# Differential heads on one Trainium2 core: all of TensorE's work in one written order

## The chip, the cores and the metric

The kernel runs on one core of one Trainium2 chip. The metric is device time in microseconds (us) of one execution. The kernel before takes 2374.95 us, the median of three runs (2369.23 to 2376.01).

The engines of the core are named as in the profile: PE is TensorE (matmuls; PEld is its weight load), DVE is VectorE, ACT is ScalarE, POOL is GpSimd, SP is SyncE, which issues the transfers. Each takes its own queue of instructions, and they wait for each other through semaphores.

## The reference

One inference step of a backbone with two layers, for 128 context tokens and 128 latent tokens, all in float32. The first layer mixes by latent and grouped-query attention, the second by differential attention; each is followed by a gated convolutional feed-forward. Every sub-layer is modulated by a shift, a scale and a gate, which are products of a condition vector with `w_ada`. The change is in the second layer's mixer (`d` is 128, 8 heads):

```python
def diff_attention(q, k, v, lam, scale):
    def block(qb):
        s = jnp.einsum("bqhjd,bkhjd->bhjqk", qb, k).astype(jnp.float32) * scale
        p = jax.nn.softmax(s, axis=-1)
        a = (p[:, :, 0] - lam * p[:, :, 1]).astype(v.dtype)
        return jnp.einsum("bhqk,bkhd->bqhd", a, v)
...
def mixer_c(h, rope, ctx, layer_idx, w_in, lq1, lk1, lq2, lk2, g_sub, w_out):
    proj = h @ w_in
    ...
    q, k = apply_rope(q, cos_h, sin_h), apply_rope(k, cos_h, sin_h)   # latent tokens only
    ...
    o = diff_attention(q, k_all, v_all, lam, HEAD_SCALE)
    o = rmsnorm(o, g_sub) * (1.0 - lambda_init)
    return o.reshape(b, t, -1) @ w_out, new_ctx
```

The context tokens attend to themselves, the latent tokens to 128 cached keys and to themselves.

## The kernel before

Both groups of tokens go through the products together, 256 columns wide (`NT`). Activations lie with features on partitions. A product is made with three matmuls for each 128x128 block of weights: the weight is split into a high part `wh` (ACT's cast, line 222) and a low part `wl` (DVE's subtraction, line 223), the activation likewise (`xh`, `xl`), and `gemm` (line 308) sums `wh*xh`, `wh*xl` (lines 317 and 318) and `wl*xh` (line 321) over 16 blocks into a PSUM bank `acc`. These 48 matmuls are a chunk. Weights arrive in 1 MB loads (`raw`, three buffers); `wh` and `wl` have four buffers of eight blocks, two chunks together, so that a cast can start when the PE has used the block that lay there two chunks earlier.

In the differential mixer (`mixer_c`, line 951) a head has six chunks: two for its queries (`dq`), two for its keys (`dk`), two for its values. The first three chunks of head 0 are made earlier by `first_three`, 45 remain. `project` (line 969) copies a chunk out of PSUM (`dev`), rotates queries and keys on DVE (`rope`, line 640), and after the values transposes them (line 993). `attend` (line 1000) is a generator, one `yield` after each part:

- scores of both halves (line 1007), the maximum `dmx` on DVE (lines 657, 658), `nmx` on POOL, the exponentials on ACT, then on DVE `drec`, `nl` and four steps on `p` (lines 1013 to 1021)
- transposes of `p` (line 672) and ACT's copy `pT`
- the product with the values, `o` (lines 1026 to 1028); its squares on ACT, three steps on POOL (`var`), the scaled `on` on DVE (line 1041)
- transposes of `on` (line 1048), and their split into `oall`

`start` runs a generator to its first `yield`, `step` takes all running ones a step further. `pump` (line 529) is called after each chunk: it calls `step`, and then, at a rate of its own, the next steps of the conditioning product (`row_step`, line 492). A unit of that product is 128x512 blocks of `w_ada`, 16 of them. Most units are made on PE (`sum_rows`, line 441). Those in `SUMMED` are summed on DVE into `aacc` (`sum_block`, lines 453 to 461, 32 steps, each kept behind the DVE instruction that was written just before it); their partitions are then summed on PE (`reduce`, line 379). Both kinds end with ACT's copy `am` (`copy`, line 386) and transposes on PE (`turn`, line 393), whose result DVE adds into `mod`; `later` holds these last steps, and each `row_step` takes one of them.

The order of an engine's queue is not the written one: a scheduler lists instructions by readiness in its own estimate and by priority. `tc.keep_in_program_order(i)` holds one instruction behind the one that was written before it on the same engine. In `gemm` before, that is done only for the chunks that are given something to do in the middle (`between`); of the mixer's chunks these are two (`todo`). All other work of PE is put where the scheduler places it, in pieces, within chunks or between them.

Of the kernel before, what the change touches and what calls it, by code (L numbers as in the profile page):

```python
# [17 lines left out]
P = 128  # L18
D = 2048
KD = D // P  # L20
T = 128
# [68 lines left out]
def step_kernel(ctx: ExitStack, tc: tile.TileContext, A: dict):  # L90
    nc = tc.nc
    pe, dve, act, pool, sp = nc.tensor, nc.vector, nc.scalar, nc.gpsimd, nc.sync
# [50 lines left out]
    def load_cw(l):  # L143
        ada["cw"] = T_(keep, [P, 4, 2 * NFF], "convw")
        tc.keep_in_program_order(sp.dma_start(out=ada["cw"], in_=A["wconv"][:, l]))
# [141 lines left out]
    def first_three(W, xh, xl, order, mid=None, fixed=False):  # L287


        pin = tc.keep_in_program_order if fixed else lambda i: i  # L290
        raws = [W.load() for _ in range(3)]
        ps = [T_(pacc, [P, 512], "acc") for _ in range(3)]
        blocks = {(c, h): W.halves(raws[c], 8 * h) for c, h in ((0, 0), (1, 0), (2, 0), (0, 1))}
        count = [0] * 3
        for n, (c, k) in enumerate(order):
            if mid and n == len(order) // 2:
                mid()
            if (c, k // 8) not in blocks:
                blocks[c, k // 8] = W.halves(raws[c], 8)
            wh, wl = blocks[c, k // 8][k % 8]  # L300
            a, b = count[c] == 0, count[c] == KD - 1
            count[c] += 1
            pin(pe.matmul(ps[c][:, :NT], wh, xh(k), start=a, stop=False))  # L303
            pin(pe.matmul(ps[c][:, :NT], wh, xl(k), start=False, stop=False))  # L304
            pin(pe.matmul(ps[c][:, :NT], wl, xh(k), start=False, stop=b))  # L305
        return [p[:, :NT] for p in ps]

    def gemm(blocks, xh, xl, n=NT, first=0, between=None):


        fixed = lambda i: tc.keep_in_program_order(i) if between else i
        ps = T_(pacc, [P, 512], "acc")
        last = len(blocks) - 1
        for i in range(last + 1):
            k = (i + first) % (last + 1)
            wh, wl = blocks[k]
            fixed(pe.matmul(ps[:, :n], wh, xh(k), start=(i == 0), stop=False))  # L317
            fixed(pe.matmul(ps[:, :n], wh, xl(k), start=False, stop=False))  # L318
# [97 lines left out]
    def load_row():  # L416
        feat["row"] = T_(feat["home"], [P, 2, D], "condb")
        sp.dma_start(out=feat["row"], in_=A["condb"])
        for r in range(2):
            tc.keep_in_program_order(act.activation(feat["row"][:, r], feat["row"][:, r], AF.Silu))  # L420

    def feature_step():
# [7 lines left out]
        tc.keep_in_program_order(dve.tensor_tensor_reduce(  # L430
# [10 lines left out]
    def sum_rows(t, raw, ps=None):  # L441
        if t == 0:
            ada["ps"] = ps or T_(ppool["ada"], [P, 512], "ada", bufs=1)
        for g in range(4):
            i = pe.matmul(ada["ps"][32 * g:32 * g + 32, :], condw[:, 4 * t + g, :], raw[:, g],  # L445
                          start=(t == 0), stop=(t == 3), skip_group_check=True)
            if pinned[0]:
                tc.keep_in_program_order(i)
# [4 lines left out]
    def sum_block(acc, block, k):  # L453
        for c in range(2):
# [6 lines left out]
            tc.keep_in_program_order(i)  # L461
# [98 lines left out]
    def modulate(hx, rb, l, which, chunks, fixed=False):  # L560


        pin = tc.keep_in_program_order if fixed else lambda i: i
# [26 lines left out]
    def modulated(st, l, which, W, fixed):  # L590
# [31 lines left out]
        def turn():  # L622
            rest[1](tc.keep_in_program_order)
# [79 lines left out]
    def mixer_ab(hx, rb0, st):  # L703
        l = 0
        with tc.tile_pool(name="ab", bufs=1) as ab:
            with tc.tile_pool(name="abp", bufs=1) as pj:
# [7 lines left out]
                def caches():  # L714
                    tc.keep_in_program_order(sp.dma_start(out=ckc, in_=A["cache_ckv"]))
                    split(kv_in[:, :, 0, T:2 * T], kv_in[:, :, 1, T:2 * T], ckc)
                    tc.keep_in_program_order(sp.dma_start(out=kr[:, T:2 * T], in_=A["cache_krope"]))
                    tc.keep_in_program_order(sp.dma_start(out=kg[:, :, T:2 * T], in_=A["cache_gqa_k"]))
                    tc.keep_in_program_order(sp.dma_start(out=vg[:, 1], in_=A["cache_gqa_v"]))
# [231 lines left out]
    def mixer_c(cp, hx, W, ready, todo, st):  # L951
# [5 lines left out]
        tc.keep_in_program_order(pe.matmul(ps[:, 0:2], ones, lm, start=True, stop=True))  # L957
# [7 lines left out]
        product = lambda: ready.pop(0) if ready else gemm(W.chunk(), xh, xl, between=todo.pop(0) if todo else None)  # L965
# [3 lines left out]
        def project(h):  # L969
# [9 lines left out]
            for dst, to in ((q, T), (k, 2 * T)):  # L979
                for i in range(2):  # L980
                    ev = T_(cp, [P, NT], "dev", bufs=2)
                    act.copy(ev, product())
                    act.copy(dst[:, i, 0:T], ev[:, 0:T])
                    rope(dst[:, i:i + 1, to:], ev[:, None, T:], 1, 64, "rch", "rsh")
                    pump(rate)
            sp.dma_start(out=A["o_diff_k"][:, 2 * h:2 * h + 2], in_=k[:, :, 0:T])
            pt = T_(ppool["att"], [P, 512], "att", bufs=3)
            for i in range(2):
                ev = T_(cp, [P, NT], "dev", bufs=2)
                act.copy(ev, product())  # L990
                pump(rate)
                for g in range(2):
                    pe.transpose(pt[:, g * NT + i * P:g * NT + (i + 1) * P],
                                 ev[:, g * T:(g + 1) * T], ident)
            act.copy(v[:, 0], pt[:, 0:NT])
            act.copy(v[:, 2], pt[:, NT:])
            sp.dma_start(out=A["o_diff_v"][:, h], in_=v[:, 0])
            return q, k, v

        def attend(h, q, k, v):  # L1000
# [15 lines left out]
            for g, ks in ((0, slice(0, T)), (1, slice(T, 3 * T))):  # L1016
# [4 lines left out]
                                         op0=ALU.mult, op1=ALU.add)  # L1021
            yield
# [21 lines left out]
            yield  # L1044
            pt = T_(ppool["att"], [P, 512], "att", bufs=3)
# [6 lines left out]

        for h in range(8):
            start(attend(h, *project(h)))
# [16 lines left out]
    def ffn(hx, W, ready, todo, l, st):  # L1071
# [4 lines left out]
        with tc.tile_pool(name=f"ffn{l}", bufs=1) as fp, banks(f"pffn{l}") as pf:  # L1076
# [4 lines left out]
            def conv(m):  # L1081
                early = bool(ready)
                pin = tc.keep_in_program_order if early else lambda i: i
# [52 lines left out]
    with banks("pab") as ppool["ada"]:  # L1136
# [4 lines left out]
        half_unit(1, 0, first[1], tc.keep_in_program_order)  # L1141
# [4 lines left out]
        half_unit(0, 0, first[0], tc.keep_in_program_order)  # L1146
# [167 lines left out]
```

## Time and profile before

| | |
|---|---|
| median of three runs | 2374.95 us |
| the profiled execution | 2372.41 us |
| its span, first to last instruction | 2370.6 us |
| its mean granted clock of TensorE | 0.993 |
| differential heads, without their first chunks and the output product | 1236 to 1545 us of the span |

The page of the profile gives busy times of whole engines, a chain of waits and groups of instructions by line; `out<-in` names the tiles that an instruction writes and reads. A view of stretches gives each engine's busy time between two times, with the number of its instructions in brackets, the granted clock (`PEclk`), the share of the DMA engines and the GB/s. A timeline gives start, duration, engine, line, operation and tiles; `x8` merges eight instructions of a line that follow each other, and square brackets show the idle time of the engine just before and what ended it. Matmuls are pipelined: the start of the next tells more than the duration. On DVE, too, the next instruction starts some 0.08 us before the profile ends the one before it.

### The profile page before, as it was taken

Reading aid. Unit: us, or ns where it says so; the run is one execution under the profiler, and the core shown is the slowest. Engines: PE = TensorE matmul, PEld = TensorE weight load, DVE = VectorE, ACT = ScalarE, POOL = GpSimd, SP = SyncE. Lnnn points to the kernel's source line nnn. Section 1 sums busy time; section 2 is a strip of 40 time slices with the busy share of each in tenths; the row PEclk is TensorE's granted clock in tenths of the full one; section 3 lists DMA queues with packets and bytes.
Section 4 is the critical chain, followed back from the end, with each engine's and each line's share of the span. In section 5 each row is a group of like instructions: output and inputs, shape, how many; then the busy total and the mean of one; then the engine's idle time right before and its main releaser. Section 6 shows DMA issues by size and latency. Waiting matters only on the chain. (4 is left out here: it accounts for less than half of the span.)

```text
span 2370.6 us, 47563 instructions
## 1 busy us (share of the span) xinstructions
PE 2312.9 (98%) x19624; PEld 2189.4 (92%) x19624; DVE 1857.6 (78%) x2886; ACT 1165.7 (49%) x1857; POOL 179.7 (8%) x210
## 2 busy tenths in 40 slices
PE   6999999999999999999999999999999999999997
PEld 4688878899999999999989999998999999999997
DVE  3569868879999999999879887888899755666654
ACT  4345544465554355554465444446555434555543
POOL 0002211200000000001220100112000000000011
PEclk9999999999999999999999999999999999999999
DMA  9988777867777877777766787777677555555553
GB/s 370 365 306 300 291 292 263 325 223 257 267 267 275 308 265 259 263 259 274 284 232 243 286 292 278 280 292 273 246 260 259 208 196 196 194 193 191 192 194 123
DMA packets 99608, 612.95 MB, mean 259 GB/s; under 512 B 10752, under 2 KB 18624, under 8 KB 29632
## 3 DMA queue, kind: packets, MB, share of 16 engines
q1 hardware_dynamic: 99392, 609.92, 70.4%
q8 instruction: 154, 2.52, 0.4%
q14 instruction: 62, 0.51, 0.1%
HBM read 605.12 MB, written 4.75 MB: 257 GB/s over the span
## 5 line engine op out<-in xcount | busy, mean ns | idle before, releaser
L222 ACT CAST wh<-raw 128x1024 fp32r<-128x1024 f32 (+1 forms) x822 | 795.6, 979 | 914.8 <-PE acc L318 745.1
L223 DVE TENSOR_TENSOR wl<-raw,wh 128x1024 fp32r<-128x1024 f32 (+1 forms) x822 | 922.0, 1138 | 312.8 <-ACT wh L222 305.9
L317 PE MATMUL acc<-hx,wh 128*128 128x256 f32 x4064 | 1131.6, 279 | 4.1 <-ACT hx L583 3.0
L321 PE MATMUL acc<-hx,wl 128*128 128x256 f32 x4064 | 1125.5, 278 | 2.5 <-DVE wl L223 2.2
L318 PE MATMUL acc<-hx,wh 128*128 128x256 f32 x4064 | 1127.0, 278 | 0.0
L317 PEld LDWEIGHTS acc<-hx,wh 128*128 128x128 f32 x4064 | 763.6, 188 | 29.8 <-issue 14.5
L321 PEld LDWEIGHTS acc<-hx,wl 128*128 128x128 f32 x4064 | 762.4, 188 | 10.9 <-issue 3.8
L318 PEld LDWEIGHTS acc<-hx,wh 128*128 128x128 f32 x4064 | 764.3, 188 | 6.7 <-issue 5.4
L318 PE MATMUL acc<-g,wh 128*128 128x256 f32 x1408 | 388.3, 276 | 0.0
L321 PE MATMUL acc<-g,wl 128*128 128x256 f32 x1408 | 388.0, 276 | 0.0
L317 PE MATMUL acc<-g,wh 128*128 128x256 f32 x1408 | 387.8, 276 | 0.0
L430 DVE CUSTOM_DVE_ANT_0 junk<-araw,condb 128x2048 f32<-128x2048 f32 x120 | 274.6, 2288 | 0.0
L318 PEld LDWEIGHTS acc<-g,wh 128*128 128x128 f32 x1408 | 264.3, 188 | 0.0
L321 PEld LDWEIGHTS acc<-g,wl 128*128 128x128 f32 x1408 | 264.2, 188 | 0.0
L317 PEld LDWEIGHTS acc<-g,wh 128*128 128x128 f32 x1408 | 264.1, 188 | 0.0
L178 POOL TENSOR_TENSOR sqacc<-sqacc,sq 128x256 f32<-128x256 f32 x62 | 82.8, 1335 | 1520.2 <-issue 1215.8
L459 DVE SCALAR_TENSOR_TENSOR aacc<-araw,condw,aacc 128x512 f32<-128x512 f32 x150 | 111.0, 765 | 0.2
L1086 ACT ACTIVATE cv<-acc,convw 128x256 f32<-128x256 f32 x176 | 98.2, 558 | 5.3 <-PE acc L305 5.3
L459 DVE SCALAR_TENSOR_TENSOR aacc<-block,condw,aacc 128x512 f32<-128x512 f32 x120 | 90.0, 780 | 6.1 <-DMA block<-w_ada 6.0
L633 DVE SCALAR_TENSOR_TENSOR x<-acc,mod,x 128x128 f32<-128x128 f32 x192 | 57.8, 342 | 39.7 <-PE acc L321 37.4
L1089 DVE SCALAR_TENSOR_TENSOR cv<-acc,convw,cv 128x254 f32<-128x254 f32 x176 | 83.4, 474 | 5.2 <-ACT cv L1086 5.1
L1092 DVE SCALAR_TENSOR_TENSOR cv<-acc,convw,cv 128x254 f32<-128x254 f32 x176 | 84.2, 479 | 3.6
(240 smaller groups left out, 1976.5 us busy)
## 6 DMA issues: line engine op xcount, KB each, us to landing
raw<-w_up SPq DMA_DIRECT2D x176, 1024.0 KB, 4.8
araw<-w_ada SPq DMA_DIRECT2D x162, 1024.0 KB, 6.2
raw<-w_down SPq DMA_DIRECT2D x88, 1024.0 KB, 4.8
raw<-w_in_c SPq DMA_DIRECT2D x48, 1024.0 KB, 5.4
raw<-w_in_ab SPq DMA_DIRECT2D x19, 1024.0 KB, 5.7
block<-w_ada SPq DMA_DIRECT2D x64, 256.0 KB, 6.1
raw<-w_out_ab SPq DMA_DIRECT2D x16, 1024.0 KB, 7.6
raw<-w_out_c SPq DMA_DIRECT2D x16, 1024.0 KB, 6.1
```

The costliest lines, as they stand in the source:

```text
L178: eng.tensor_tensor(out=st["acc"], in0=st["acc"], in1=sq, op=ALU.add)
L222: pin(act.copy(out_hi, src))
L223: pin(dve.tensor_tensor(out=out_lo, in0=src, in1=out_hi.bitcast(F32), op=ALU.subtract))
L317: fixed(pe.matmul(ps[:, :n], wh, xh(k), start=(i == 0), stop=False))
L318: fixed(pe.matmul(ps[:, :n], wh, xl(k), start=False, stop=False))
L321: fixed(pe.matmul(ps[:, :n], wl, xh(k), start=False, stop=(i == last)))
L430: tc.keep_in_program_order(dve.tensor_tensor_reduce(out=T_(feat["pool"], [P, D], "junk"), in1=feat["row"][:, c], in0=feat["raw"].rearrange ...
L459: i = dve.scalar_tensor_tensor(out=acc[c], in0=block, scalar=condw[:, k, c:c + 1], in1=acc[c], op0=ALU.mult, op1=ALU.add)
L633: dve.scalar_tensor_tensor(out=x[:, c, s], in0=ps[:, s], scalar=mod[:, l, 3 * which + 2, c, g:g + 1], in1=x[:, c, s], op0=ALU.mult, op1=AL ...
L1086: pin(act.activation(y, ps, AF.Identity, scale=cw[:, 1, m:m + 1], bias=cw[:, 3, m:m + 1]))
L1089: pin(dve.scalar_tensor_tensor(out=y3[:, :, 1:], in0=p3[:, :, :T - 1], scalar=cw[:, 0, m:m + 1], in1=y3[:, :, 1:], op0=ALU.mult, op1=ALU.add))
L1092: pin(dve.scalar_tensor_tensor(out=y3[:, :, :T - 1], in0=p3[:, :, 1:], scalar=cw[:, 2, m:m + 1], in1=y3[:, :, :T - 1], op0=ALU.mult, op1=A ...
```

## The change

All of PE's instructions go through a small class. While `in_turn` is set, over the eight heads, each is kept behind the one written before it. `keep_order` is the old call, made once for an instruction. Each chunk of the mixer now has a `between`: in its middle come, in this order, what `todo` holds, `pump`, and what `soon` holds (the start of a head's `attend`, in its last value chunk). `attend` gets the value transposes as a part of its own, and one more `yield` before the last part, so that a head's steps stand in the middles of six chunks: scores, value transposes, transposes of `p`, `o`, none, transposes of `on`. `dev` has five buffers instead of two, since the value copies live longer.

```diff
-    pe, dve, act, pool, sp = nc.tensor, nc.vector, nc.scalar, nc.gpsimd, nc.sync
+    dve, act, pool, sp = nc.vector, nc.scalar, nc.gpsimd, nc.sync
+    kept = []
+
+    def keep_order(i):
+        if not any(i is j for j in kept):
+            kept[:] = [i]
+            tc.keep_in_program_order(i)
+
+    class TensorE:
+        in_turn = False
+        def matmul(self, *a, **kw):
+            return self.placed(nc.tensor.matmul(*a, **kw))
+        def transpose(self, *a, **kw):
+            return self.placed(nc.tensor.transpose(*a, **kw))
+        def placed(self, i):
+            if self.in_turn:
+                keep_order(i)
+            return i
+
+    pe = TensorE()
...
-        product = lambda: ready.pop(0) if ready else gemm(W.chunk(), xh, xl, between=todo.pop(0) if todo else None)
+        soon = []
+
+        def product(rate):
+            def middle():
+                if todo:
+                    todo.pop(0)()
+                pump(rate)
+                while soon:
+                    soon.pop(0)()
+            return ready.pop(0) if ready else gemm(W.chunk(), xh, xl, between=middle)
...
             for dst, to in ((q, T), (k, 2 * T)):
                 for i in range(2):
-                    ev = T_(cp, [P, NT], "dev", bufs=2)
-                    act.copy(ev, product())
+                    ps = product(rate)
+                    ev = T_(cp, [P, NT], "dev", bufs=5)
+                    act.copy(ev, ps)
                     act.copy(dst[:, i, 0:T], ev[:, 0:T])
                     rope(dst[:, i:i + 1, to:], ev[:, None, T:], 1, 64, "rch", "rsh")
-                    pump(rate)
             sp.dma_start(out=A["o_diff_k"][:, 2 * h:2 * h + 2], in_=k[:, :, 0:T])
-            pt = T_(ppool["att"], [P, 512], "att", bufs=3)
+            evs = []
             for i in range(2):
-                ev = T_(cp, [P, NT], "dev", bufs=2)
-                act.copy(ev, product())
-                pump(rate)
-                for g in range(2):
-                    pe.transpose(pt[:, g * NT + i * P:g * NT + (i + 1) * P],
-                                 ev[:, g * T:(g + 1) * T], ident)
-            act.copy(v[:, 0], pt[:, 0:NT])
-            act.copy(v[:, 2], pt[:, NT:])
-            sp.dma_start(out=A["o_diff_v"][:, h], in_=v[:, 0])
-            return q, k, v
+                if i:
+                    soon.append(lambda: start(attend(h, q, k, v, evs)))
+                ps = product(rate)
+                ev = T_(cp, [P, NT], "dev", bufs=5)
+                act.copy(ev, ps)
+                evs.append(ev)
 
-        def attend(h, q, k, v):
+        def attend(h, q, k, v, evs):
...
             yield
+            pt = T_(ppool["att"], [P, 512], "att", bufs=3)
+            for i, ev in enumerate(evs):
+                for g in range(2):
+                    pe.transpose(pt[:, g * NT + i * P:g * NT + (i + 1) * P],
+                                 ev[:, g * T:(g + 1) * T], ident)
+            act.copy(v[:, 0], pt[:, 0:NT])
+            act.copy(v[:, 2], pt[:, NT:])
+            sp.dma_start(out=A["o_diff_v"][:, h], in_=v[:, 0])
+            yield
             pT = transposed(cp, pj[0])
...
             yield
+            yield
             pt = T_(ppool["att"], [P, 512], "att", bufs=3)
...
+        pe.in_turn = True
         for h in range(8):
-            start(attend(h, *project(h)))
+            project(h)
+        pe.in_turn = False
         flush()
```

Elsewhere `tc.keep_in_program_order` becomes `keep_order`, with the same effect.

More of the change, by code (lines that the diff above doesn't have):

```diff
@@ L956, in mixer_c @@
         ps = att_bank()
-        tc.keep_in_program_order(pe.matmul(ps[:, 0:2], ones, lm, start=True, stop=True))
+        keep_order(pe.matmul(ps[:, 0:2], ones, lm, start=True, stop=True))
         ex = T_(cp, [P, 2], "ex")
@@ L1082, in conv @@
                 early = bool(ready)
-                pin = tc.keep_in_program_order if early else lambda i: i
+                pin = keep_order if early else lambda i: i
                 ps = product()
```

30 lines of the change are left out of this document (15 added, 15 removed).

## The prediction

> **What bounds the kernel now.** I read the page first.
>
> ```profile
> span 2370.6 us, 47563 instructions
> PE 2312.9 (98%) x19624; PEld 2189.4 (92%) x19624; DVE 1857.6 (78%) x2886; ACT 1165.7 (49%) x1857; POOL 179.7 (8%) x210
> PE 30%; issue 0%; DVE 0%; POOL 0%; ACT 0%; DVEq 0%; POOLq 0%; ACTq 0%
> ```
>
> TensorE (PE) is never out of work: busy 98%, and the only engine of weight on the chain that ended last. The change touches the differential heads, so the second view is the busy time by stretches: the whole stage, then the four stretches in which VectorE (DVE) sums a conditioning unit (`aacc`, lines 456 and 459), and one stretch between two of them.
>
> ```profile
> core 0: us, PE busy (x) PEld busy (x) DVE busy (x) ACT busy (x) POOL busy (x), PEclk, DMA share, GB/s
> 1236.00:1545.00 309.00, 309.00 (x2573) 287.94 (x2575) 252.27 (x456) 148.21 (x303) 26.56 (x40) 1.00 0.76 274
> 1251.32:1299.23 47.91, 47.91 (x415) 47.65 (x414) 47.22 (x82) 24.59 (x46) 2.93 (x5) 1.00 0.70 252
> 1299.23:1325.35 26.12, 26.12 (x206) 20.79 (x206) 14.20 (x27) 11.43 (x28) 2.55 (x5) 1.00 0.87 309
> 1325.35:1371.00 45.65, 45.65 (x391) 45.39 (x389) 45.34 (x80) 22.61 (x44) 4.77 (x5) 1.00 0.74 268
> 1398.70:1444.50 45.80, 45.80 (x386) 45.44 (x385) 45.48 (x80) 23.69 (x47) 5.43 (x6) 1.00 0.70 253
> 1472.10:1518.00 45.90, 45.90 (x391) 45.64 (x390) 45.49 (x82) 21.53 (x43) 4.05 (x5) 1.00 0.76 270
> ```
>
> PE is busy in every microsecond, so it waits for nothing here. But in the four summing stretches DVE is as full as PE: a unit takes DVE 46 to 48 us, whatever PE does. Between them DVE is half idle (14.20 of 26.12). PE does not wait only because what it needs from DVE stands late enough in its queue. The third view, DVE's timeline for one head inside such a stretch, shows how late, and gives the prices.
>
> ```profile
> 1277.34 1.47 PE L1007 MATMUL att<-dk,dq 128*128 128x128 f32 x8
> 1278.76 0.28 PE L318 MATMUL acc<-hx,wh 128*128 128x256 f32 x1
> ...
> 1279.65 0.28 DVE L657 TENSOR_REDUCE dmx<-att 128x1 f32<-128x128 f32 x1
> 1279.85 0.41 DVE L658 TENSOR_REDUCE dmx<-att 128x1 f32<-128x256 f32 x1
> 1280.18 1.21 DVE L223 TENSOR_TENSOR wl<-raw,wh 128x1024 fp32r<-128x1024 f32 x1
> ...
> 1285.75 0.17 DVE L1013 RECIPROCAL drec<-dsums 128x4 f32<-128x4 f32 x1
> ...
> 1287.72 0.59 DVE L648 TENSOR_TENSOR rope<-dev,cst 64x128 f32<-64x128 f32 x2
> 1288.32 0.29 DVE L650 TENSOR_TENSOR dq<-dev,cst 128x128 f32<-128x128 f32 x1
> 1288.53 0.74 DVE L459 SCALAR_TENSOR_TENSOR aacc<-araw,condw,aacc 128x512 f32<-128x512 f32 x1
> 1289.19 0.22 DVE L1015 TENSOR_SCALAR nl<-drec,nlam 128x2 f32<-128x2 f32 x1
> ...
> 1289.98 1.22 DVE L223 TENSOR_TENSOR wl<-raw,wh 128x1024 fp32r<-128x1024 f32 x1
> 1291.12 0.28 DVE L651 TENSOR_TENSOR dq<-dq,rope 128x128 f32<-128x128 f32 x1
> ...
> 1291.99 0.54 DVE L1017 TENSOR_SCALAR p<-p,nl 128x128 f32<-128x128 f32 x2
> ...
> 1295.83 0.74 DVE L1019 SCALAR_TENSOR_TENSOR p<-p,drec,p 128x128 f32<-128x128 f32 x2
> 1296.48 0.75 DVE L459 SCALAR_TENSOR_TENSOR aacc<-araw,condw,aacc 128x512 f32<-128x512 f32 x1
> ...
> 1299.60 0.41 PE L379 MATMUL ada<-aacc,cst 128*32 128x256 f32 x2
> ```
>
> Scores at 1277.34, the finished weights `p` at 1296.48: 19 us, over three chunks, since DVE takes its queue in turn. The sum of the unit is read by PE (line 379) at 1299.60, just as DVE ends it. From start to start the prices on DVE are: `aacc` step 0.66 (1288.53 to 1289.19), `wl` 1.14, a `dmx` pair 0.53, a `rope` pair 0.60, one `dq` or `dk` 0.21, the four `p` steps 1.11 (0.65 and 0.54 less the 0.08 by which neighbours overlap), `drec` and `nl` 0.22. As a test, the built order has 4 `dmx`, 5 `wl`, 10 `aacc`, 2 `rope` pairs, 3 `dq`, `drec`, `nl` and 4 `p` in this chain: 1.06 + 5.70 + 6.60 + 1.20 + 0.63 + 0.22 + 1.11 = 16.5 us, against 16.8 in the rows (1279.65 to 1296.48).
>
> **The change, part by part.** The written order is now PE's order. In the built program a chunk is 26 matmuls, one interruption, 22 matmuls; 76 interruptions over the stage become 42. Work is neither added nor removed: 2160 chunk matmuls in both. PE's prices:
>
> ```profile
> 1267.90 0.28 PE L317 MATMUL acc<-hx,wh 128*128 128x256 f32 x1
> ...
> 1272.66 0.28 PE L317 MATMUL acc<-hx,wh 128*128 128x256 f32 x1
> ```
> ```profile
> 1253.55 0.59 PE L1026 MATMUL att<-dv,pT 128*128 128x256 f32 x2
> ...
> 1254.96 0.28 PE L318 MATMUL acc<-hx,wh 128*128 128x256 f32 x1
> ```
> ```profile
> 1257.46 0.88 DVE L1041 SCALAR_TENSOR_TENSOR on<-att,var,cst 128x256 f32<-128x256 f32 x2 [0.28 <-POOL var L1038]
> ```
> ```profile
> 1260.30 0.60 PE L1048 MATMUL att<-cst,on 128*128 128x128 f32 x4
> 1260.66 0.37 PE L317 MATMUL acc<-hx,wh 128*128 128x256 f32 x1
> 1260.87 0.28 PE L318 MATMUL acc<-hx,wh 128*128 128x256 f32 x1
> ```
>
> 42 matmuls from 1267.90 to 1272.66 give 0.113 us each: 5.44 a chunk, 2.95 to its interruption, 2.49 after it. Scores cost 1.30 (1277.34 to 1278.76 less one matmul), `o` 1.30, four transposes 0.46. From the start of `o` to `on` on DVE it is 3.9 us (1253.55 to 1257.46, through ScalarE and three POOL steps); the `on` pair holds DVE 0.80.
>
> **Fewer interruptions.** A return to the chunk costs a matmul about 0.21 instead of 0.11 (1260.66 to 1260.87). If all 34 that go cost that, 3.4 us are saved; if the work merely moves, 0. I take 2.
>
> **Steps in turn on PE: the waits.** Anything that PE reaches before its operand is ready now holds back every matmul behind it. I set DVE's built order against PE's from a point where DVE must wait for PE (`dmx` after the first half of the scores, 0.65; `on` after `o`) to the point where PE needs DVE. `oall` (128x512) is taken as half a `wl`, 0.60.
>
> - Unit 1, its sum read in the first chunk of head 2. DVE from `on`: 0.80, 22 `aacc` 14.5, 8 `wl` 9.1, 2 `rope` pairs 1.2, 4 `dk` 0.8, `oall` 0.6, 4 `dmx` 1.06, `drec` and `nl` 0.22, 2 `p` 0.5: 28.8. PE from `o`: 1.30 + 2.49, 5.44, 5.44 + 0.46, 2.95 + 1.30 + 2.49, 2.95 + 0.46 = 25.3, less the 3.9 before `on`: 21.4. Wait 7.4.
> - Unit 3, the same places with 24 `aacc` and 4 `p`: 30.8 against 21.4. Wait 9.4.
> - Unit 2, first at `p` (second chunk of head 3): DVE 1.06, 5 `wl` 5.7, 10 `aacc` 6.6, 0.22, 0.6, 0.2, 1.11 = 15.5; PE 0.65 + 2.49 + 5.44 + 0.46 + 2.95 = 12.0. Wait 3.5. Then at the sum, from `p`: `o` after 0.35 + 2.49 + 2.95 = 5.8, `on` 3.9 later at 9.7, then 0.8, 8 `aacc` 5.3, 2 `wl` 2.3, 0.6, 0.4: 19.1; PE is there at 5.8 + 1.30 + 2.49 + 2.95 = 12.5. Wait 6.6.
> - Unit 4, first at `p`, 4 `wl` instead of 5: 14.4 against 12.0. Wait 2.4. Then at the sum: 9.7 + 0.8, 8 `aacc` 5.3, 4 `wl` 4.6, 1.2, 0.6, then `oall`, `dk` and 2 `aacc` 2.1: 24.3; PE 12.5 + 2.49 + 2.95 + 0.46 = 18.4 (one chunk later, behind the transposes of `on`). Wait 5.9.
>
> Together 35.2 us. What stands behind each wait is the chunk itself and, through the weight buffers that it frees, ScalarE's casts and SyncE's loads, so nothing else fills the time. In the old order PE's queue had the first unit's sum three chunks later, at the end of head 2's keys.
>
> **Copy and turn in one interruption.** In four interruptions the sum, ScalarE's copy of it (`am`) and the transposes of the copy now follow each other. The nearest row is the same sequence early in the program:
>
> ```profile
> 98.87 0.66 PE L393 MATMUL ada<-cst,am 128*128 128x128 f32 x4 [0.71 <-ACT am L386]
> ```
>
> ```profile
> 1287.22 1.06 ACT L222 CAST wh<-raw 128x1024 fp32r<-128x1024 f32 x1 [0.96 <-PE acc L318]
> ```
>
> 4 x 0.71 = 2.8, which I take, as ScalarE is half idle in this stage; if each copy first waits for a cast, 4 x 1.77 = 7. Below 0 it cannot come, since the transposes need the copy.
>
> **The clock after a wait.** PE's granted clock falls after an idle stretch:
>
> ```profile
> 1192.36:1195.78 3.42, 2.05 (x22) 1.95 (x24) 2.17 (x6) 1.46 (x3) 0.00 (x0) 1.00 0.30 71
> 1195.78:1199.19 3.41, 3.41 (x14) 0.80 (x18) 1.03 (x4) 0.00 (x0) 0.70 (x1) 0.50 0.87 198
> ```
>
> A window with 1.37 us idle was followed by 3.41 us at half clock, in which 1.7 us of progress are lost if PE has work. After the first waits of units 2 and 4 DVE uses that time and the second wait shrinks; four ends are left: 0 to 6.8, and 4 taken, as part of a half-clock window falls inside the wait. The Trainium skill (TensorE: Matmul & The Clock Gate, Part 1) says that the clock halves after at least one idle window of about 3.4 us. By that page the 2.4 us wait would cost no clock; the trace is stricter, since a window that was 60% busy sufficed, and I go by it.
>
> **The rest.** The value transposes move into `attend`, one chunk after the copies that feed them: covered by half a chunk, 2.95, against a copy and at most one cast of 1.06 before it; without that cover 0.71 each, as for `am` above. `dev` grows to five buffers, which nothing waits for. The `o_diff_v` store moves with the transposes and waits on SyncE a chunk later; weight loads behind it lie two chunks ahead. Together 0 to 3, taken 0.
>
> **Sum.** 35.2 + 2.8 + 4 - 2 = +40 on the profiled execution's 2372.4 us (span 2370.6): 2412. The runs' median, 2375, lies 2.5 above that execution; I leave that in the range.
>
> **Rivals.**
> - *Only what DVE is short of counts.* If DVE finds work during the 3.9 us to `on`, a unit waits only for the difference over its whole length. Unit 1: DVE 32 `aacc` 20.6, 15 `wl` 17.1 and 9.7 of small steps, 47.4; PE six chunks 32.6, their interruptions 3.9, the rest of the first 4.3 and the half of the last 3.4, 44.2. In the same way units 2 to 4: 40.4 against 31.7, 40.2 against 34.2, 42.4 against 37.1. Together 23 us; with 3 for the copies and less 2: 2396. For it: DVE had no idle time in the old stretches. Against: each `aacc` is kept behind the `on` that precedes it.
> - *Clock and late weights add up.* Every one of six waits is followed by a half-clock window that no later wait takes back (10), and `wl` waits a cast of 1 us more in each (6): 2424 to 2430.
> - *No wait, not slower.* DVE starts each unit in its slack (12 us in 1299.23 to 1325.35) early enough to be done when PE asks. Gain alone: 2369 to 2372. It decides only if starts move forward by 6 to 10 us a unit, or an `aacc` step took 0.66 - 35.2/84 = 0.24 us. The built order holds the first `aacc` behind `wl` and `dk` that depend on a chunk just ended.
> - *Slow pace.* After some interruptions matmuls keep a slower pace:
>
> ```profile
> 1405.57 0.28 PE L317 MATMUL acc<-hx,wh 128*128 128x256 f32 x1
> ...
> 1408.75 0.28 PE L317 MATMUL acc<-hx,wh 128*128 128x256 f32 x1
> ```
>
> 27 in 3.18 us, 0.118 each. All 2160 at it cost under 10 us more; with no waits 2379.
>
> **How the numbers follow.** Forecast 0.55 (2400 to 2424), shortage only 0.20, clock and late weights 0.14, no wait 0.06, slow pace without waits 0.05. The range 2385 to 2430 takes in the first three but for their tails. A measurement of this kernel cannot tell 0.3% (7 us) from no change. The case without waits is split between faster (0.04) and same, the slow pace is same (together 0.07), all else slower: 0.89.
>
> **What would show it.** PE idle, 30 to 45 us, in six places before `ada<-aacc` and `att<-cst,p`, released by DVE; about 0.7 before `ada<-cst,am`; half-clock windows behind them; DVE's chains of 12 to 31 us at the same prices as here. It is wrong if PE stays busy over the stage, if the waits lie elsewhere (scores, weights), or if DVE's order on the chip lets PE through sooner.

## The result, and the profile after

The changed kernel takes 2426.95 us (median of 4 runs, 2425.24 to 2428.14), the kernel before, in the same comparison, 2374.67 (2369.23 to 2376.01): a ratio of 1.0226, interval 1.0214 to 1.0239. The change makes it 52 us slower. The page of the changed kernel's profiled execution, whose own time is 2425.24:

```profile
span 2423.5 us, 47544 instructions
PE 2325.9 (96%) x19624; PEld 2198.9 (91%) x19624; DVE 1859.8 (77%) x2886; ACT 1167.7 (48%) x1857; POOL 175.6 (7%) x210
PE 29%; issue 0%; DVE 0%; POOL 0%; ACT 0%; DVEq 0%; POOLq 0%; ACTq 0%
```

The same 19624 matmuls keep PE busy 13.0 us longer (2325.9 against 2312.9), and the span grows by 52.9. So most of the growth is time in which PE does nothing, and a part is the same work at a slower pace. Next the stage of the heads, from the first product of the differential mixer to the last product with `oall`, as busy time by stretches; first the kernel before, one row, in the columns that the prediction shows:

```profile
1222.03:1625.24 403.21, 402.60 (x3373) 375.69 (x3372) 330.03 (x582) 193.56 (x373) 43.19 (x54) 1.00 0.76 276
```

Then the changed kernel, the stage and the four stretches from the first `aacc` step of a unit to its last:

```profile
1222.17:1676.72 454.55, 414.64 (x3373) 383.37 (x3372) 331.09 (x582) 194.87 (x373) 38.78 (x54) 0.96 0.67 245
1237.29:1291.49 54.20, 45.98 (x384) 44.58 (x383) 47.97 (x86) 24.85 (x52) 4.22 (x7) 0.97 0.64 229
1322.68:1367.21 44.53, 34.28 (x273) 33.13 (x271) 41.02 (x72) 17.43 (x35) 2.88 (x5) 0.92 0.64 233
1398.22:1440.55 42.33, 33.06 (x278) 31.31 (x270) 40.72 (x72) 17.33 (x36) 2.89 (x5) 0.94 0.71 260
1473.81:1522.34 48.53, 39.33 (x314) 37.84 (x312) 43.22 (x77) 19.30 (x38) 1.98 (x5) 0.95 0.65 238
```

The stage is 51.3 us longer, with the same 3373 matmuls: PE idle rises from 0.6 to 39.9, and its busy time by 12.0, at a mean granted clock of 0.96. DVE's work hardly changes (330.0 and 331.1). All but 1.6 us of the longer span lies in this stage. The view of waits names what PE waited for in it (us in total, times, longest):

```profile
PE ada L105 <- DVE aacc L482: 26.1, 4, 8.6
PE att L108 <- DVE p L1049: 10.0, 3, 4.3
PE ada L108 <- ACT am L409: 2.4, 4, 0.7
```

(In the changed kernel every matmul is recorded at line 105 and every transpose at 108, the two lines of the new class.) The four sums, three waits for `p`, four short ones for `am`: the places that the prediction named, and one more, `p` in the first head (1.6 us). One of them, unit 3's sum, in PE's timeline:

```profile
1430.42 0.28 PE L105 MATMUL acc<-hx,wl 128*128 128x256 f32 x1
1430.54 0.40 PE L105 MATMUL acc<-hx,wh 128*128 128x256 f32 x2
1430.78 0.60 PE L108 MATMUL att<-cst,dev 128*128 128x128 f32 x4
1439.94 1.73 PE L105 MATMUL ada<-aacc,cst 128*32 128x256 f32 x8 [8.57 <-DVE aacc L482]
1441.60 0.58 PE L105 MATMUL acc<-hx,wl 128*128 128x256 f32 x1
...
1442.41 0.41 PE L105 MATMUL acc<-hx,wl 128*128 128x256 f32 x1
...
1443.05 0.41 PE L105 MATMUL acc<-hx,wl 128*128 128x256 f32 x1
```

and in DVE's:

```profile
1433.44 1.23 DVE L246 TENSOR_TENSOR wl<-raw,wh 128x1024 fp32r<-128x1024 f32 x1
...
1435.37 1.41 DVE L482 SCALAR_TENSOR_TENSOR aacc<-araw,condw,aacc 128x512 f32<-128x512 f32 x2
...
1438.48 0.75 DVE L1049 SCALAR_TENSOR_TENSOR p<-p,drec,p 128x128 f32<-128x128 f32 x2
1439.14 1.41 DVE L482 SCALAR_TENSOR_TENSOR aacc<-araw,condw,aacc 128x512 f32<-128x512 f32 x2
```

PE arrives at 1431.38. DVE works without a gap until the unit's last two steps, which start at 1439.14, with a `wl` and the head's `p` in between. PE does nothing meanwhile: the rest of the chunk stands behind the sum in its queue, and goes on at 1441.60 with no wait of its own. A matmul then takes 0.41 us (1442.41) where one before the wait took 0.28 (1430.42), and three start in 0.64 us (1442.41 to 1443.05). The reason stands in the windows of 3.41 us in which the granted clock (the column behind POOL) changes:

```profile
1428.50:1431.91 3.41, 2.88 (x25) 2.64 (x23) 3.41 (x6) 3.31 (x11) 0.71 (x2) 1.00 0.53 216
1431.91:1435.33 3.42, 0.00 (x0) 0.00 (x0) 3.42 (x7) 1.11 (x3) 0.00 (x0) 1.00 0.44 89
1435.33:1438.74 3.41, 0.00 (x0) 0.00 (x0) 3.41 (x8) 0.00 (x0) 0.00 (x0) 0.50 0.98 394
1438.74:1442.16 3.42, 2.22 (x10) 0.93 (x11) 1.81 (x4) 0.37 (x1) 0.00 (x0) 0.50 0.56 196
1442.16:1445.57 3.41, 3.41 (x18) 3.41 (x17) 0.00 (x0) 0.00 (x0) 0.00 (x0) 0.50 0.68 281
1445.57:1448.98 3.41, 3.41 (x32) 3.41 (x31) 1.66 (x3) 1.74 (x4) 0.00 (x0) 1.00 0.00 0
```

Each window with much idle time is followed by one at half clock; this wait brings three. The stage has 37.5 us at half clock after, none before, and PE is busy in 25.8 of them. If work takes twice as long there, half of that, 12.9 us, is lost. Measured is a busy time 12.0 longer: either about 0.8 comes back elsewhere, or the work takes a little less than twice as long; these runs don't tell the two apart.

### The profile page after: what moved, and what is told of

Its sections match the earlier page's. It is cut to its first block, busy times and chain, and to the rows that moved or that the text cites. A ratio compares the mean times of both kernels' runs of the same rounds, so it can differ in the third digit from the quotient of the medians.

```text
span 2423.5 us, 47544 instructions
## 1 busy us (share of the span) xinstructions
PE 2325.9 (96%) x19624; PEld 2198.9 (91%) x19624; DVE 1859.8 (77%) x2886; ACT 1167.7 (48%) x1857; POOL 175.6 (7%) x210
## 5 line engine op out<-in xcount | busy, mean ns | idle before, releaser
L105 PE MATMUL acc<-hx,wh 128*128 128x256 f32 x8416 | 1464.6, 279 | 10.1 <-ACT hx L606 4.5
L105 PEld LDWEIGHTS acc<-hx,wh 128*128 128x128 f32 x8416 | 1278.7, 189 | 45.5 <-issue 15.8
L105 PE MATMUL acc<-hx,wl 128*128 128x256 f32 x4208 | 1172.6, 280 | 3.4 <-DVE wl L246 3.2
L105 PEld LDWEIGHTS acc<-hx,wl 128*128 128x128 f32 x4208 | 794.9, 189 | 22.0 <-issue 10.0
L105 PE MATMUL acc<-g,wh 128*128 128x256 f32 x2816 | 478.8, 276 | 0.0
L105 PEld LDWEIGHTS acc<-g,wh 128*128 128x128 f32 x2816 | 423.9, 188 | 0.0
L105 PE MATMUL ada<-araw,condw 128*32 128x512 f32 (+1 forms) x608 | 76.1, 585 | 19.2 <-DMA araw<-w_ada 17.8
L105 PE MATMUL acc<-oall,wh 128*128 128x256 f32 x512 | 90.3, 280 | 0.8 <-ACT oall L245 0.7
L105 PEld LDWEIGHTS acc<-oall,wh 128*128 128x128 f32 x512 | 78.1, 189 | 2.1 <-ACT oall L245 0.9
L105 PE MATMUL acc<-oall,wl 128*128 128x256 f32 x256 | 71.1, 279 | 0.0
```

The costliest lines, as they stand in the source:

```text
L105: return self.placed(nc.tensor.matmul(*a, **kw))
```

## The experiments

The theory: the 52 us are waits of a PE that may not step aside, for a DVE that is full while it sums a unit, and the half-clock windows behind them. Its rivals: the longer route of a head, the one interruption a chunk, or the plain lack of DVE time. In the diffs "-" is the changed kernel (or the one named), "+" the experiment. Idle time in the stage means gaps of more than 0.15 us between PE's instructions, added up.

### The written order taken away

```diff
-        pe.in_turn = True
         for h in range(8):
             project(h)
...
-            return ready.pop(0) if ready else gemm(W.chunk(), xh, xl, between=middle)
+            return ready.pop(0) if ready else gemm(W.chunk(), xh, xl, between=middle, pinned_=bool(todo))
```

> The changed kernel's loops, its one interruption a chunk and its later value transposes stay, but TensorE's instructions in the heads are no longer held to the written order (only a chunk that carries a `todo` keeps its matmuls together). Theory (the 52 us are waits of TensorE for a VectorE that is full, made by the written order, and the half-clock windows behind them): the built order again moves each unit's sum some three chunks on, the six waits before `ada<-aacc` and `att<-cst,p` go, no half-clock window is left in the stage, and the time is 2371 to 2379 us. Rival 1 (the longer route of a head itself, six chunks with the turns later, costs time): 2390 us or more with TensorE idle elsewhere. Rival 2 (the one interruption a chunk with both sums and turns in it is what stalls): waits of about 0.7 before `ada<-cst,am` and some of the 4 to 8 us ones remain, 2400 us or more.

2372.52 us, 1.0005 of before [0.9995, 1.0014]. The stage, as busy time by stretches:

```profile
1224.85:1627.78 402.93, 402.65 (x3374) 376.14 (x3372) 328.21 (x582) 193.80 (x373) 50.82 (x54) 1.00 0.75 276
```

Next to no idle time (0.3 us), full clock. And unit 1's sum with that head's `p`, in PE's timeline:

```profile
1284.55 0.38 PE L108 MATMUL att<-cst,dev 128*128 128x128 f32 x2
...
1299.57 0.62 PE L105 MATMUL ada<-aacc,cst 128*32 128x256 f32 x4
...
1301.66 0.27 PE L108 MATMUL att<-cst,p 128*128 128x128 f32 x1
```

DVE ends the unit at 1300, much where it ended it before the change; PE reads it at once, having filled the 14 us since the value transposes with chunks. So the written order costs the 52 us: a head's new layout, left to the scheduler, costs nothing that can be measured, nor does it gain. DVE isn't short of time as such either, with 328.2 us of work in 402.9. The one interruption a chunk isn't tested here, since the scheduler breaks the chunks up again: between the mixer's first product and the first one with `oall`, other work interrupts PE's chunks 77 times before, 43 times in the changed kernel, and 77 times in this one.

### The written order alone

The kernel before, with its own order held (in "-" and "+" here, against the kernel before):

```diff
+        pe.in_turn = True
         for h in range(8):
             start(attend(h, *project(h)))
+        pe.in_turn = False
```

> The kernel before with one thing changed: TensorE's instructions in the heads are held to its own written order. The head's steps are not spread: the value transposes stand right behind the chunk whose copy they need, `p` is turned one chunk after the scores rather than two, and the unit's sum is at its old written place. Theory (the written order costs, and the spreading over six chunks takes some of that back): waits of about 1 us before each of 16 value transposes (16 to 25 us), at `p` about 5.4 us more than in the changed kernel in each head with a unit (9 us, four times) and some 1 to 3 us in the others, the sums' waits smaller by as much as `p` waited, and half-clock windows behind most: 2450 to 2500 us. Rival (the spreading is what put the steps at places where VectorE is late): no slower than the changed kernel, 2427 us or less.

2438.2 us in a single run, 12 below the expected span but 11 above the changed kernel. The waits:

```profile
PE att L108 <- DVE p L1042: 16.4, 4, 6.8
PE ada L105 <- DVE aacc L482: 15.1, 3, 7.8
PE att L108 <- ACT dev L1013: 10.5, 11, 1.3
```

Spreading the head takes away the waits for `dev` (10.5) and some of those for `p`, while those at the sums grow from 15.1 to 26.1; it doesn't take away the cause. The waits for `p` came out smaller than reckoned, as I read it because every earlier wait gives DVE time.

### The units summed by TensorE

```diff
-SUMMED = [22, 24, 26, 28, 31]
+SUMMED = [31]
```

> The written order is kept, but the conditioning units 22, 24, 26 and 28 are summed by TensorE (16 products with the conditioning columns each, line 468) instead of VectorE (`aacc`); unit 31 stays. VectorE loses 4 x 32 steps of 0.66 us, 84 us. Theory (a full VectorE is what TensorE waits for): the waits before `att<-cst,p` and the sums go, TensorE gets 4 x 16 matmuls of 512 columns, some 4 us a unit, 16 in all, and the copies' waits of 0.7 stay: 2390 to 2400 us with no wait of over 2 us in the stage. Rival (the waits come from the chain of one head, score to `p`, being too long for the chunks between, whatever VectorE holds beside it): waits of 3 to 4 us before `att<-cst,p` in several heads, 2415 us or more.

2408.85 us, 1.0153 of before [1.0136, 1.017], 9 above the expected span, and waits of over 2 us are left. The waits:

```profile
PE att L108 <- DVE p L1049: 5.3, 1, 5.3
PE ada L105 <- DVE mod L425: 5.2, 8, 1.3
PE ada L105 <- DVE aacc L482: 5.0, 1, 5.0
```

Where TensorE sums, no wait exceeds 1.3 us. The two long ones belong to the one unit left on DVE, which this kernel reaches before the end of the heads: 10.3 us for a single unit, beside a unit's 7 to 10 in the changed kernel. PE's added work costs 15.1 us (stage less idle less clock loss, 417.7 against 402.6). So a DVE that sums a unit is a condition of the long waits.

### `p` later, sums later, both

`p` later: one more `yield` ahead of the transposes of `p`. Sums later: twelve empty steps ahead of `reduce`, and a bank of its own. These are steps of the side plan, several to an interruption: unit 1's sum is asked 75.2 us into the stage instead of 62.1.

```diff
             sp.dma_start(out=A["o_diff_v"][:, h], in_=v[:, 0])
             yield
+            yield
```
```diff
-        return ([reduce] if on_dve else []) + [copy, turn]
+        wait = [lambda: None] * 12 if on_dve and acc is None and pe.in_turn else []
+        return wait + ([reduce] if on_dve else []) + [copy, turn]
```

> The changed kernel with one edit: `p` is turned one chunk later (5.4 us), and all that follows it in a head; the sums stay where they were. Theory: no wait before `att<-cst,p`; the four sums wait as in the changed kernel, longer in the second and fourth unit by what `p` waited before (6.6, 9 to 10, 8.6, 8 to 9 us), 30 to 34 us idle, 8 to 12 us lost to the clock behind them: 2408 to 2418 us. Rival (moving `p` cuts the chain on which the sum waits, since `on` stands in VectorE's queue ahead of `aacc`): VectorE ends the units earlier and the sums wait half as long, 2390 to 2400 us.

> The written order is kept, but the two things that TensorE asked of VectorE too early are written later: the sum of each of units 1 to 4 twelve interruptions later (three chunks and more), in a bank of its own, and the transposes of `p` with all that follows them one chunk later. Work, durations and the order on TensorE between these are those of the changed kernel. Theory (not the written order as such, but the place at which it asks, costs the time): all six long waits go, and with them every half-clock window; left are four waits of about 0.7 for `am`, or fewer, and the small gain of the fewer interruptions (0.6): 2372 to 2380 us. Rival (a written order in which nothing can step aside stalls wherever it is put, on scores, casts or weights): the waits move to other operands and the time stays over 2390 us.

`p` later: 2416.42 us, 1.0189 [1.0175, 1.0203], as the theory has it, though the four sums wait a little less than it says (5.5, 8.4, 7.4 and 7.1 us). Its waits:

```profile
PE ada L105 <- DVE aacc L482: 28.6, 5, 8.4
```

Both later: 2391.8 us, 1.0081 [1.0066, 1.0096]. All waits of the changed kernel at sums and at `p` are gone, with as few interruptions as there (40, counted as above), so that these aren't where the six long waits came from. But the expected 2372 to 2380 isn't reached. What the rival forecast is there: the waits moved to another operand, and the time is over 2390, if barely:

```profile
PE ada L105 <- DMA araw<-w_ada: 13.5, 4, 4.8
PE ada L108 <- ACT am L409: 1.4, 2, 0.7
```

The new wait stands at the next unit's first products. After unit 2, in PE's timeline:

```profile
1352.03 0.39 PE L105 MATMUL acc<-hx,wh 128*128 128x256 f32 x2
1355.94 1.94 PE L105 MATMUL ada<-araw,condw 128*32 128x512 f32 x8 [3.52 <-DMA araw<-w_ada]
```

and in the queue of SyncE:

```profile
1347.83 0.38 SPq L532 DMA_DIRECT2D araw<-w_ada  x1
```

The load is issued at 1347.83, when DVE has done with the third of the unit's four raw blocks and one of the two `araw` buffers is free, and lands 8.1 us later. PE asks at 1352.4. Here it is the same late DVE, reached through a buffer. The other three loads were late in other ways. Those behind units 1 and 4 were issued when PE had used a block of its own (1290.83 and 1494.31), at a time when DVE still held the second buffer. The one behind unit 3 stood in SyncE's queue behind a weight load that waited for a `wl`, and was issued at 1417.01.

The next edit was to let PE multiply the raw blocks later. In its first form it stood in a branch that the heads don't take (`pinned` is still set), so that two kernels ran without it: one is the last kernel over again, the other has the sums late and `p` at its old place.

> The kernel with sums and `p` asked late, in which the waits of 1.8, 3.5, 3.4 and 4.8 us that were left stood before `ada<-araw,condw`, the products of the next unit, whose raw block was still on its way. One more thing is asked later: a unit that TensorE sums multiplies each raw block four side steps (some 8 us) after it did, within the same two buffers. Theory (those loads were late because VectorE, behind by then, freed `araw` late; what costs is still only TensorE's asking too early): these four waits and the three pairs of half-clock windows go, waits of about 0.7 for `am` stay, 2371 to 2379 us, the same as before. Rival (the written order passes each wait on to the next operand, so that VectorE's lag is paid somewhere): 10 us or more idle in other places of the stage, 2385 us or more.

> Sums and raw blocks asked late as in the kernel before this one, but `p` again at the changed kernel's place, two chunks after the scores. Theory (two separate questions to a full VectorE): waits stay before `att<-cst,p` alone, about 1.6 in the first head, 4.3 and 4.1 in the second and fourth unit and 2 to 3.5 in the other two (there the changed kernel's waits at the sum came first and gave VectorE time), 12 to 16 us idle, with half-clock windows behind those in which two idle us fall into one window: 2386 to 2395 us. Rival (the wait at `p` is itself a result of the wait at the sum): 2380 us or less.

The repetition gave 2391.66 us, 1.0083 [1.0068, 1.0098], with waits at the same four places. Its instructions on PE and on DVE stand in the same order throughout, yet its profiled execution has 14.8 us idle in the stage and 13.7 at half clock, the first one 16.1 and 20.5: so far two executions of one program differ. Sums late alone gave 2410.57, 1.0168 [1.0152, 1.0184], 16 above the expected span:

```profile
PE att L108 <- DVE p L1059: 20.9, 5, 5.5
PE ada L105 <- DMA araw<-w_ada: 4.8, 2, 3.9
```

With nothing ahead of it `p` waits in five heads: 1.6, 5.5, 4.3, 5.4 and 4.1 us. In units 1 and 3 of the changed kernel the wait at the sum had hidden it. Each set against before in its own comparison, `p` later takes off 7 us of the 52, sums later 13, both 33: more than the two together, for each wait gives DVE the time that the other then needs less.

Then the edit in the branch that is taken, on the kernel with both late (`lag` is set for units that begin within the heads):

```diff
-            if g == 1 and t:
+            if g == (3 if ada["lag"] else 1) and t:
                 sum_rows(t - 1, ada["last"])
...
-                    later.append(lambda: None)
+                    later.extend([lambda: None] * (3 if ada["lag"] else 1))
```

> The kernel with sums and `p` asked late, and here with the raw blocks asked later in the branch that the heads do take (`pinned`, lines 536 to 544): a block is multiplied at the fourth side step of the next block, not at the second, and the last at the fourth step of what follows. Two side steps are some 4 to 5 us, a little more than the waits of 3.4 to 4.8 us that stood before `ada<-araw,condw`. Theory (only asking too early costs): the four waits shrink to 1 us or less each, no half-clock window is left behind them, 2372 to 2382 us. Rival (a block multiplied later frees its buffer later, so the next load is late by as much): the waits move on to the second or third block of the unit and 8 us or more idle stay, 2384 us or more.

2390.21 us, 1.0076 [1.0063, 1.009]; 16.0 us idle, as before the edit. The waits:

```profile
PE ada L105 <- DMA araw<-w_ada: 7.4, 4, 3.9
PE att L108 <- DVE on L1084: 3.3, 1, 3.3
PE att L108 <- DVE p L1052: 2.0, 2, 1.1
```

The rival is right: what one place no longer waits, others do.

### Only the heads in written order

The unit's work on PE (raw blocks, sums, turn) is no longer held itself, with `p` late and with `p` as in the changed kernel (`sum_rows`, too, holds its products only where `free` isn't set):

```diff
     def row_step(until=len(ROWS)):
+        ada["free"], pe.in_turn = pe.in_turn, False
+        row_steps(until)
+        ada["free"], pe.in_turn = False, ada["free"]
```

> The written order of the changed kernel is kept for the chunks and the steps of the heads, with `p` asked one chunk later, but the conditioning units' work on TensorE (raw blocks, sums, the turn of `am`) is left to the scheduler, as before the change. It puts the sum of the first unit two and a half chunks after where the changed kernel has it, those of the others one to two and a half. Theory: with the sum behind VectorE's end and `p` a chunk later nothing waits for VectorE by more than about 3 us, and few windows run at half clock: 2372 to 2385 us. Rival (a partly written order still makes TensorE wait for the unit, since the scheduler reckons VectorE faster than it is): sums wait 3 us or more in three or four units, 2390 us or more.

> As the last kernel, but `p` at the changed kernel's place: only the units' work on TensorE is left to the scheduler. Theory: what stays are the waits before `att<-cst,p` that the run with the sums late showed (1.6, 5.5, 4.3, 5.4 and 4.1 us, 21 in all) with some 6 to 8 us lost to the clock behind them: 2396 to 2406 us, and no wait of over 2 us before a sum or a raw block. Rival (without the sums' places in the written order VectorE's queue is built otherwise, and `p` stands earlier in it): 2385 us or less.

2418.01 us, 1.0188 [1.0174, 1.0202], and 2427.98, 1.0232 [1.0218, 1.0246]: the same times and waits as with these places written (2416.42 and 2426.95). The view of waits of the first, to be set beside `p` later above:

```profile
PE ada L105 <- DVE aacc L483: 28.6, 5, 8.4
```

The expectation misread the built order: the sums hadn't moved. Of PE's 19624 matmuls 8 stand elsewhere than in the kernels with these places written, raw blocks' products that went ahead of value transposes; nothing went later. That fits the call: it holds an instruction behind the one written before it, and the chunk's next matmul, still held, has the unit's sum before it. So this edit lets a unit's work step forward, but lets no chunk pass it, and what the heads alone in written order would cost stays untested.

### DVE's share of a unit

Steps of units that DVE sums at 1.25 of their spacing, of the others at 0.8, on the changed kernel and on the one with both late:

```diff
-            ada["due"] -= 0.25 if dve_or_none else 0.25 * ada["pew"]
+            slow = (1.25, 0.8) if pe.in_turn else (1.0, 1.0)
+            ada["due"] -= 0.25 * slow[0] if dve_or_none else 0.25 * ada["pew"] * slow[1]
```

> The changed kernel with one number of its side plan altered: in the heads a step of a unit that VectorE sums is paced at 1.25 of the old spacing, a step of a unit that TensorE sums at 0.8, so that the same units are done in the stage with the first kind spread over some 7.7 interruptions instead of 6.2. The written order and all places in a head stay. A unit then has some 8 us more of TensorE's time, of which VectorE needs about 4 for the chunks' `wl` and small steps in it. Theory (a unit's 47 us of VectorE work are more than the written order gives it): the sums' waits fall by 3 to 5 us each, to 1.5 to 5, those at `p` by about 1.3 (two `aacc` steps fewer ahead of it), 13 to 20 us idle in all and about 5 lost to the clock: 2388 to 2400 us. Rival (the waits are set by the chain of one head and the place of the ask, not by the share of VectorE that a unit takes): 35 us or more idle, 2418 us or more.

> The same pacing on the kernel with sums and `p` asked late, whose four waits of 1.8 to 4.8 us at raw blocks were left because VectorE, still behind at the end of a unit, freed those buffers late. Theory (with VectorE no longer full in a unit the written order costs nothing): these waits go, 6 us idle or less and at most two half-clock windows in the stage, 2371 to 2381 us. Rival (TensorE's four raw blocks, now closer together on two buffers, wait for their own loads): 10 us or more idle before `ada<-araw,condw`, 2385 us or more.

On the changed kernel 2417.56 us, 1.0182 [1.0166, 1.0198]:

```profile
PE att L108 <- DVE p L1050: 18.8, 4, 5.4
PE ada L105 <- DVE aacc L482: 6.8, 4, 3.9
```

The sums' waits fall from 26.1 to 6.8, as the theory has it, but those for `p` rise from 10.0 to 18.8, nearly what they were with the sums late (20.9), and the time is far over the expected 2388 to 2400: a head's chain from scores to `p` is too long for two chunks in a head with a unit, at this pacing too. And 32 us idle, now in waits of 4 to 5 us, bring 44 us at half clock, more than the changed kernel's 37.5. On the other kernel 2388.23 us, 1.0063 [1.0049, 1.0076], the fastest with a written order, but over the expected 2371 to 2381, and with waits for raw blocks, as the rival has it (9.1 us, it has 10 or more):

```profile
PE ada L105 <- DMA araw<-w_ada: 9.1, 4, 3.9
PE att L108 <- DVE on L1083: 2.3, 1, 2.3
```

Together, from the profiled executions (us; the difference is of medians in one comparison):

| TensorE's order in the heads | against before | idle in the stage | stage time at half clock, busy or idle |
|---|---|---|---|
| changed kernel | +52.3 | 39.7 | 37.5 |
| not written | +0.2 | 0.3 | 0 |
| written, heads not spread (one run) | +65.9 | 51.2 | 44.4 |
| units summed by PE (15.1 more work) | +36.5 | 18.7 | 10.2 |
| `p` later | +45.3 | 33.0 | 41.0 |
| units evened out | +44.5 | 32.2 | 44.4 |
| sums later | +39.4 | 27.8 | 30.7 |
| both later | +19.5 | 16.1 | 20.5 |
| both later, raw blocks later | +17.9 | 16.0 | 13.7 |
| both later, units evened out | +15.2 | 12.8 | 10.2 |

The last three rows differ by little more than two executions of one program do (above). No kernel here beats the one before. Whether a written order without waits exists stays open: three placements with both later were tried, and each left 12.8 us idle or more.

## Why the prediction was right, and where not

The changed kernel is slower, as forecast, and 2426.95 lies within the range of 2385 to 2430. But it is 15 us above the sum's 2412 and outside the 2400 to 2424 that got the largest chance: the waits were worked out rightly, the clock behind them was not. That the range takes the time in is owed to the room it left for the rival *Clock and late weights add up*.

- *What bounds the kernel now*: right. DVE is full in the summing stretches, and PE was spared only because it could ask late. Taking the order away gives back all of it; taking the sums off DVE takes away the long waits.
- *Steps in turn on PE: the waits*: right in place and size. Predicted 7.4, 3.5 + 6.6, 9.4, 2.4 + 5.9, in all 35.2; measured 6.6, 4.3 + 5.9, 8.6, 4.1 + 5.1, in all 34.5. Unit 3 shows why: from `on` to the unit's end DVE took 31.1 us (1409.45 to 1440.55; 30.8 by the count), and PE came to the sum 25.7 after `o` (25.3). The prices stayed the same: a `wl` takes 1.23 in the timeline above, 1.22 before. What was left out is the first head, whose `p` waited 1.6: unit 1 starts there, at 1237.29, 14 us earlier than before the change.
- *Copy and turn in one interruption*: 2.8 predicted, 2.4 in the row for `am`. Two of the four waits stand behind DVE's sums (0.47 each, units 1 and 4), the other two behind units that PE sums (0.7 each); after units 2 and 3 the turn came an interruption later and waited for no copy. *The rest*: 1.2 us for one `oall` and for two waits on `mod` were not in the sum.
- *Fewer interruptions*: the count was right (76 to 42; 77 to 43 as counted above). 2 us were to be gained; in the stage it is about 0.8 at most, as said above, and the kernel without the order, with its 77 interruptions, can't tell. The lower end of its bounds was nearer.
- *The clock after a wait*: this is the term that was mis-sized, 4 taken and 12.9 measured (12.0 by the longer busy time). The step thought of one half-clock window behind a wait, part of it inside the wait. But a wait of 5 to 9 us reaches over two or three windows, each of which is answered by one at half clock, and the last of these fall on work; and the waits for `p` of units 2 and 4, which it took to cost nothing, had half-clock windows too. At the six waits these come to 6.8, 3.4, 6.8, 10.2, 3.4 and 6.8 us. The term explains 8.9 of the 12.8 us by which the profiled execution passed the sum (52.8 against 40); the first head, the smaller gain and the `oall` and `mod` waits explain 4.0, the waits and copies that came out smaller take 1.1 off, and about 1 us is left, outside the stage.
- The trace decided rightly against the Trainium skill (TensorE: Matmul & The Clock Gate, Part 1), by which the clock halves after at least one idle window of about 3.4 us. No window at unit 2's wait for `p` was idle throughout, and the clock halved:

```profile
1343.17:1346.58 3.41, 0.34 (x2) 0.15 (x2) 3.41 (x7) 0.00 (x0) 0.00 (x0) 1.00 0.98 411
1346.58:1349.99 3.41, 3.41 (x16) 3.41 (x17) 3.41 (x7) 0.48 (x1) 0.00 (x0) 0.50 0.37 154
```

- Of the rivals, *Clock and late weights add up* (2424 to 2430) had the time, for half of its reason: the clock lost 12.9 where it has 10, but nothing in the view of waits is a late weight, for which it has 6. *Only what DVE is short of counts* fell: 34.5 us were waited, not 23. *No wait, not slower* fell, and its remark that the steps would have to start earlier is of use: unit 1 did start 14 us earlier, and DVE spent the time, 54.2 us for the unit. *Slow pace* fell: of the intervals between a head's chunk matmuls 713 are of 0.115 to 0.130 us before and 520 after.

## What to carry to other kernels

An order written out on the bounding engine turns every lag of the engines that feed it into idle time, even if these have slack on the average: count, from the prices in the trace, the feeding engine's queue from where it gets its input to where the bounding engine asks, and put the ask behind that, buffers and loads included. None of the placements tried here did so without new waits. Two asks on the same full engine hide each other, so that moving one shows less than it costs. For TensorE add the clock to each wait of over 2 us: here 39.7 us of waits cost another 12 to 13.

## What the runs showed of the hardware

Over the fourteen traces of this case, from 60 us on, I set each window of 3.41 us against the granted clock of the next. From full clock: less than 1.0 us idle, never half (9147 windows); 1.0 to 1.97, half in 47 of 148; 1.97 or more, half in 82 of 82. At half clock already, less idle time keeps it there: 0.8 us or more did so in all 49 windows, less in 12 of 131. So a window need not be idle throughout, and at half clock an idle time of 0.8 to 1.0 us keeps it there, which from full clock never brought it about. Between 1.0 and 2.0 us it comes more often the longer the idle time: 7 of 55 below 1.25 us, 18 of 52 to 1.5, 10 of 25 to 1.75, 12 of 16 above. What else decides there wasn't tried.
